# Partial sums kept in the inner tiles of the feed-forward layers, two products of the second tile pair ahead, splits issued in order, lo parts of projection weights by adding transfers

## The chip, the cores and the metric

The kernel runs on one core of a Trainium2 chip (trn2). The metric is the device time of one execution in microseconds (us); lower is better. A run's time is compared by the median of several executions.

## The reference

One inference step of one layer, in float32, over 512 prompt frames and 64 sample frames, which the kernel handles as one matrix of T = 576 tokens with D = 1024 features:

```python
h = layer_norm(ALPHA * x + 0.5 * swiglu_ffn(x, ffn1_w_gu, ffn1_w_down))       # FFN1, LN1
z = h @ w_in            # mLSTM q, k, v, o, i, f | attention q, k, v | gates g_ml, g_att
y_ml  = (normed mLSTM(q, k, v, i, f) * sigmoid(o)) @ w_ml_proj
y_att = band_attention(q, k, v) @ w_att_proj
h = layer_norm(ALPHA * h + (sigmoid(g_ml) * y_ml + sigmoid(g_att) * y_att) @ w_out)   # LN2
y = layer_norm(ALPHA * h + 0.5 * swiglu_ffn(h, ffn2_w_gu, ffn2_w_down))       # FFN2, LN3

def swiglu_ffn(x, w_gu, w_down):
    gate, up = jnp.split(x @ w_gu, 2, axis=-1)
    return (jax.nn.silu(gate) * up) @ w_down          # 2816 hidden features = 22 tiles
```

## The kernel before, in words

**Operands.** Every fp32 operand of a matmul is split in two: `hi`, the operand rounded to the type fp32r, and `lo` = operand − `hi`. A product is three matmuls: hi·hi, hi·lo, lo·hi. ACT makes the `hi` (helper `act`, L137), DVE the `lo` (helper `tt`, L140; `stt`, L143, where a sign is turned).

**Stages.** FFN1, LN1, the projections with the mixers, LN2, FFN2, LN3. The projections run in this order: attention v, k, q for eight pairs of heads (weight tiles 48+j, 40+j, 32+j of `w_in`), attention's gates (64 to 71), its output projection (`ap`), the mLSTM's four heads with eight tiles each (0 to 31), its gates (56 to 63), its output projection (`mp`), the merged output projection (`o`). The tiles `ap`, `mp`, `o` and the gates run back to back on TensorE; between the tiles of the pairs and heads TensorE also runs the mixer.

**Weight stream.** `pump` (L183) keeps a list `plan` of weight tiles of 128x1024. SP loads a raw tile (`wr`, 2 buffers), ACT writes `wh`, DVE writes `wl` = `wr` − `wh` (L213 to 216); `wh` and `wl` have NWB = 4 buffers, so the split of a tile begins when TensorE has finished the tile four before. Four gate/up tiles of FFN2 are split ahead of time by `early` (L172) during the last projection: their `lo` is made by ACT as −hi, and a DMA issued by POOL (L180) adds the raw weights from DRAM onto it (`el`, `eh`).

**The inner tiles of an FFN.** Of the 22 hidden tiles the first two (FFN1) or three (FFN2) are plain. From j = CL on, gate and up tile are made together in Winograd's form of Strassen's scheme (class `Units`, L625): seven products of 12 matmuls of 288 tokens each, in place of eight. Its operands are quarters of the input and sums of them (class `Combos`, `make`, L593: t1 to t4 for four pairs of k-tiles, called as the first unit begins), and quarters of the weights a11, a12, a22 and sums of them s1 to s4 (`prep`). In `run`, the products of one unit j come in this order on TensorE:

- a11·b11 into the PSUM bank X, whose value is copied to `e1` in SBUF,
- a12·b21 into a bank Y; `h` = silu(Y + `e1`) is the gate's first half,
- s2·t2 added onto X, copied to `e2`,
- s1·t1 into Z, s3·t3 onto X, copied to `e3`; `c22` = −`e3` − Z,
- in `finish`, a22·t4 onto X and s4·b22 onto Z, and the rest of the gate and up halves.

The first two products need only the inputs as they are (b11, b21); s2·t2 is the first product that needs a sum of inputs. In the names below `mm_540` is the first unit's bank X in FFN1, `s_495`, `s_512` and so on are hi parts of sums t, `s_496`, `s_513` their lo parts, `tt` the sum itself, `ws`, `wt` the sums of weights, `wu` the raw weights of a unit.

**The down projection.** Output tiles 0 and 1 run together (`joined`), over the hidden tiles that `Hidden.upto` (L762) splits; `get` asks for four ahead.

**What sets the order.** TensorE's order is the program's: `Order.later` puts closures of other work between the matmuls. ACT, DVE, POOL and SP are ordered by a list scheduler with priorities (`hot(n)`, `tc.high_priority(offset=n)`); each of them then runs its list in order.

Of the kernel before, what the change touches and what calls it, by code (L numbers as in the profile page):

```python
# [17 lines left out]
P = 128  # L18
# [63 lines left out]
def tile_layer(ctx: ExitStack, tc: tile.TileContext, ins, outs):  # L82
# [73 lines left out]
    WARM = 8  # L156
    LAST = {1: 6, 2: 6}
    CL = {1: 2, 2: 3}
    NX = 8
    NH0 = 1  # L160
    PIECES = {("in", 48), ("in", 40), ("in", 32)}

    EARLY = [("gu2", j, e) for j in range(2) for e in range(2)]
    CP = (6, 7)
# [4 lines left out]
    wst = {"dma": 0, "conv": 0, "taken": 0, "used": 0, "stop": 0}  # L169
    raws, parts = {}, {}  # L170

    def early(pool, key):  # L172
        c = [k for k, _ in plan].index(key)
        raw = wpool.tile([P, 1024], F32, tag="wr", name=nm("wr"), bufs=2)
        SP.dma_start(raw, plan[c][1])
        hi, lo = parts[c] = tuple(pool.tile([P, 1024], F32R, tag=t, name=nm(t), bufs=len(EARLY)) for t in ("eh", "el"))
        act(hi, raw)

        act(lo, f(hi), scale=-1.0)
        POOL.dma_start(lo, plan[c][1], accum_op=ALU.add)  # L180

    @hot(30)
    def pump(limit=2):  # L183
        while True:
            c = wst["conv"]
            if wst["dma"] < len(plan) and plan[wst["dma"]][0] in EARLY:
                wst["dma"] += 1
                continue
            if c < len(plan) and plan[c][0] in EARLY:
                assert c in parts  # L190
                wst["conv"] += 1
                continue
            if wst["dma"] < min(len(plan), c + 2):
                i = wst["dma"]
                raws[i] = wpool.tile([P, 1024], F32, tag="wr", name=nm("wr"), bufs=2)
                src = plan[i][1]
                SP.dma_start(raws[i][:, :src.shape[1]], src)
                wst["dma"] += 1
                continue
            if c < wst["stop"] and c < wst["taken"] + limit and wst["used"] < NWB:  # L200
                raw = raws.pop(c)
                n = plan[c][1].shape[1]
                hi = wpool.tile([P, 1024], F32R, tag="wh", name=nm("wh"), bufs=NWB)
                if plan[c][0] == "if":

                    r3 = raw[:, :n].rearrange("p (k c) -> p k c", c=64)
                    h3 = hi.rearrange("p (k c) -> p k c", c=P)
                    act(h3[:, :, 0:64], r3)
                    tt(h3[:, :, 64:128], r3, f(h3[:, :, 0:64]), ALU.subtract)
                    parts[c] = (hi, None)  # L210
                else:
                    lo = wpool.tile([P, 1024], F32R, tag="wl", name=nm("wl"), bufs=NWB)
                    step = n if plan[c][0] not in PIECES else 512  # L213
                    for a in range(0, n, step):
                        act(hi[:, a:a + step], raw[:, a:a + step])
                        tt(lo[:, a:a + step], raw[:, a:a + step], f(hi[:, a:a + step]), ALU.subtract)
                    parts[c] = (hi, lo)
                wst["used"] += 1
                wst["conv"] += 1
                continue  # L220
            return
# [411 lines left out]
    class Units:  # L633
# [55 lines left out]
                       skip_group_check=True)  # L689
                od.tick()  # L690

        def copy(self, ps, tag, bufs):
            e = self.pool.tile([P, HT_], F32, tag=tag, name=nm(tag), bufs=bufs)
            act(e, ps)
            return e

        def run(self, tail):
            cur = None
            for j in self.js + [None]:
                new = None  # L700
                if j is not None:
                    new = dict(j=j, X=bank("mm")[:, :HT_], h=self.hr.tile([P, T], F32, tag="h", name=nm("h"), bufs=FT + 1))
                    self.product(new["X"], j, "a11", "b11", True, False)
                    with tc.high_priority(offset=60):
                        new["E1"] = self.copy(new["X"], "e1", 1)
                if cur is not None:
                    self.finish(cur)
                if j is None:
                    return
                h = new["h"]  # L710

                def first(new=new, j=j, h=h):
                    Y = bank("mm")[:, :HT_]
                    self.product(Y, j, "a12", "b21", True, True)
                    with tc.high_priority(offset=60):
                        tt(h[:, :HT_], Y, new["E1"], ALU.add)
                        act(h[:, :HT_], h[:, :HT_], AF.Silu)

                if j < FT - 1:
                    first()  # L720
                else:
                    tail()
                self.prep(j + 1, "a")
                self.prep(j + 1, "s")
                self.product(new["X"], j, "s2", "t2", False, False)
                with tc.high_priority(offset=60):
                    new["E2"] = self.copy(new["X"], "e2", 2)
                self.prep(j + 1, "t")
                Z = new["Z"] = bank("mm")[:, :HT_]
                self.product(Z, j, "s1", "t1", True, False)  # L730
                self.product(new["X"], j, "s3", "t3", False, False)
                with tc.high_priority(offset=60):
                    e3 = self.copy(new["X"], "e3", 1)
                    c = new["c"] = self.pool.tile([P, HT_], F32, tag="c22", name=nm("c22"), bufs=1)
                    stt(c, e3, -1.0, Z, ALU.mult, ALU.subtract)
                self.prep(j + 1, "u")
                if j == FT - 1:
                    first()
                cur = new

        def finish(self, u):
            j, h = u["j"], u["h"]
            self.product(u["X"], j, "a22", "t4", False, True)
            with tc.high_priority(offset=60):
                stt(h[:, :HT_], u["X"], -1.0, h[:, :HT_], ALU.mult, ALU.mult)
            self.prep(j + 1, "b")
            self.load(j + 3)
            self.product(u["Z"], j, "s4", "b22", False, True)
            with tc.high_priority(offset=60):
                tt(h[:, HT_:], u["Z"], u["E2"], ALU.add)  # L750
                act(h[:, HT_:], h[:, HT_:], AF.Silu)
                tt(h[:, HT_:], h[:, HT_:], u["c"], ALU.mult)
            self.hr_done(j, h)

    class Hidden(Act):


        def __init__(self, raw, pools):
            super().__init__()
            self.raw, self.pools = raw, pools  # L760

        def upto(self, k):  # L762
            while len(self.p) <= min(k, FT - 1):
# [1 line left out]
                pool, tag, n = self.pools[(j >= NH0) + (j >= FT // 2)]  # L765
                hi = pool.tile([P, T], F32R, tag=tag, name=nm(tag), bufs=n)
                lo = self.spare if j == FT // 2 - 1 else pool.tile([P, T], F32R, tag=tag, name=nm(tag), bufs=n)
                act(hi, self.raw[j])
                tt(lo, self.raw[j], f(hi), ALU.subtract)
                self.p.append((hi, lo))  # L770

        def get(self, k, hf):
# [829 lines left out]
```

## Time and profile before

| | us |
|---|---|
| median of 3 runs (lowest, highest) | 1629.75 (1627.64, 1630.14) |
| the profiled execution, time | 1625.21 |
| its span on the core | 1623.4 |
| busy: PE, DVE, ACT, POOL | 1585.7, 1082.9, 816.2, 139.0 |
| TensorE's mean granted clock | 0.991 of full |

The span is the time from the first to the last instruction. Busy times are sums over the span; an engine that is less busy than another can still be the one that the other waits for in one place. In the timelines a row's bracket tells how long the engine was idle before it, and what ended that.

### The profile page before, as it was taken

The page shows a single profiled execution, that of the slowest core. Times are in us where ns is not written, and L with a number is a line of the kernel's source. Part 1 is how long each engine was busy: PE and PEld are TensorE (multiplying, and loading weights), DVE is VectorE, ACT ScalarE, POOL GpSimd, SP SyncE. Part 2 cuts the span into 40 slices and gives each one's busy share as a digit, 9 for nine tenths or more (in the row PEclk, how much of TensorE's full clock was granted, in tenths as well). Part 3 has the DMA queues.
Part 4 walks back from the last instruction along what each step waited for, and adds up shares of the span by engine and source line. Part 5 has one row for each costly group of instructions (what it writes and reads, how often), then busy time and mean ns, then how long its engine had stood idle before and what let it go on. Part 6 is the DMA issues. An engine that isn't in the chain of part 4 may idle for free.

```text
span 1623.4 us, 29315 instructions
## 1 busy us (share of the span) xinstructions
PE 1585.7 (98%) x11831; PEld 1561.3 (96%) x11831; DVE 1082.9 (67%) x2154; ACT 816.2 (50%) x1529; POOL 139.0 (9%) x277
## 2 busy tenths in 40 slices
PE   9899999999999999999999999999998999999997
PEld 8899999999999999999999999999998999999996
DVE  7777777635787777673757658434787677766636
ACT  6455456223566566651657476533454455445223
POOL 0000000000313223000101101002110000000001
PEclk9899999999999999999999999999999999999998
DMA  6122231234332333122222122222522232212333
GB/s 217 53 104 104 80 105 46 89 90 124 120 126 87 100 107 102 45 88 85 79 72 79 60 88 64 79 73 84 146 76 78 79 105 93 90 65 85 88 90 116
DMA packets 52896, 148.61 MB, mean 92 GB/s; under 512 B 5784, under 2 KB 16664, under 8 KB 52760
## 3 DMA queue, kind: packets, MB, share of 16 engines
q1 hardware_dynamic: 51608, 144.11, 27.4%
q0 software_dynamic: 576, 2.10, 0.8%
q8 instruction: 93, 1.52, 0.4%
q10 hardware_dynamic: 576, 0.52, 0.1%
q14 instruction: 43, 0.35, 0.1%
HBM read 137.47 MB, written 9.24 MB: 90 GB/s over the span
## 4 chain that ended last, share of the span: by engine, by line
PE 54%; DVE 4%; ACT 1%; issue 1%; DMA 1%; POOL 1%; ACTq 0%; SPq 0%; POOLq 0%; DVEq 0%
PE mm L123 47%; PE aux L123 5%; PE aux L133 1%; DVE s L140 1%; DVE wl L140 1%; DVE s L143 1%; DMA wr<-in_w_gu 1%; ACT wh L137 0%; ACT s L137 0%; DVE tt L140 0%; DMA wr<-in_w_o 0%; DVE dg L140 0%; POOL kh L147 0%; DVE ptl L140 0%; ACT sc L137 0%
## 5 line engine op out<-in xcount | busy, mean ns | idle before, releaser
L123 PE MATMUL mm<-s,wh 128*128 128x288 f32 (+2 forms) x3900 | 799.8, 299 | 13.2 <-ACT s L137 11.5
L123 PEld LDWEIGHTS mm<-s,wh 128*128 128x128 f32 x3900 | 627.9, 190 | 18.4 <-ACT s L137 12.3
L123 PE MATMUL mm<-s,wl 128*128 128x288 f32 (+2 forms) x1934 | 572.4, 296 | 0.0
L123 PEld LDWEIGHTS mm<-s,wl 128*128 128x128 f32 x1934 | 366.5, 189 | 0.0
L140 DVE TENSOR_TENSOR wl<-wr,wh 128x1024 fp32r<-128x1024 f32 (+2 forms) x162 | 192.9, 1195 | 185.3 <-ACT wh L137 184.9
L137 ACT ACTIVATE wh<-wr 128x1024 fp32r<-128x1024 f32 (+2 forms) x163 | 164.7, 1014 | 285.9 <-PE mm L123 267.9
L123 PE MATMUL mm<-h,wh 128*128 128x256 f32 (+1 forms) x672 | 134.5, 294 | 0.0
L140 DVE TENSOR_TENSOR wl<-ws,wh 128x1024 fp32r<-128x1024 f32 x39 | 47.8, 1226 | 112.4 <-ACT wh L137 112.4
L123 PE MATMUL mm<-hc,wh 128*128 128x320 f32 (+1 forms) x560 | 113.7, 295 | 4.8 <-ACT hc L137 2.9
L123 PEld LDWEIGHTS mm<-h,wh 128*128 128x128 f32 x672 | 107.5, 187 | 0.2
L123 PE MATMUL mm<-tx,wh 128*128 128x288 f32 x468 | 98.1, 299 | 1.8 <-ACT e L137 1.8
L123 PE MATMUL mm<-h,wl 128*128 128x256 f32 (+1 forms) x336 | 98.6, 293 | 0.0
L123 PEld LDWEIGHTS mm<-hc,wh 128*128 128x128 f32 x560 | 90.1, 188 | 5.7 <-ACT hc L137 3.4
L137 ACT ACTIVATE wh<-ws 128x1024 fp32r<-128x1024 f32 x39 | 41.2, 1057 | 102.7 <-PE mm L123 102.7
L123 PE MATMUL mm<-hc,wl 128*128 128x256 f32 (+1 forms) x280 | 82.6, 295 | 0.0
L123 PEld LDWEIGHTS mm<-tx,wh 128*128 128x128 f32 x468 | 76.6, 192 | 2.0 <-ACT e L137 2.0
L432 POOL TENSOR_TENSOR rs<-var,mhalf 128x2 f32<-128x2 f32 (+1 forms) x6 | 5.2, 864 | 823.9 <-DVE var L143 428.0
L123 PE MATMUL mm<-tx,wl 128*128 128x288 f32 x234 | 69.9, 299 | 0.0
L123 PEld LDWEIGHTS mm<-h,wl 128*128 128x128 f32 x336 | 62.9, 187 | 0.0
L137 ACT ACT_TABLE_LOAD x45 | 57.7, 1283 | 7.4 <-DVE U L143 4.0
L137 ACT ACTIVATE e<-mm 128x288 f32<-128x288 f32 x117 | 47.3, 404 | 22.6 <-PE mm L123 22.4
L137 ACT ACTIVATE wh<-wu 128x1024 fp32r<-128x1024 f32 x39 | 41.4, 1061 | 31.9 <-PE mm L123 31.9
(297 smaller groups left out, 3061.9 us busy)
## 6 DMA issues: line engine op xcount, KB each, us to landing
wu<-in_w_gu SPq DMA_DIRECT2D x78, 512.0 KB, 4.3
wr<-in_w_in SPq DMA_DIRECT2D x72, 512.0 KB, 3.5
wr<-in_w_dn SPq DMA_DIRECT2D x40, 512.0 KB, 3.5
wr<-in_w_dn SPq DMA_DIRECT2D x20, 384.0 KB, 3.1
G<-in_rbias SPq DMA_DIRECT2D x16, 256.0 KB, 2.8
wr<-in_w_ap SPq DMA_DIRECT2D x8, 512.0 KB, 3.5
wr<-in_w_mp SPq DMA_DIRECT2D x8, 512.0 KB, 3.4
wr<-in_w_o SPq DMA_DIRECT2D x8, 512.0 KB, 3.5
```

What stands on the lines that cost most here:

```text
L123: PE.matmul(out, lhsT, rhs, start=start, stop=stop, **kw)
L133: PE.transpose(out, in_, idn)
L137: ACT.activation(out, in_, func, **kw)
L140: return (eng or DVE).tensor_tensor(out, a, b, op=op)
L143: DVE.scalar_tensor_tensor(out=out, in0=a, scalar=s, in1=b, op0=op0, op1=op1)
L432: return y, POOL.tensor_tensor(y, v, mhalf[:, :n], op=ALU.pow)
```

## The change

1. `add_lo`: for 90 weight tiles (the set `ADDED`: attention's tiles of pairs 2 to 7, the 32 of the mLSTM, the 16 gates, `ap`, `mp`, `o`) `pump` has ACT write `wl` = −`wh` and POOL issue a DMA that adds the raw weights from DRAM, in place of DVE's subtraction.
2. The copies of X go into the halves of `h` and into `c22`, in place of `e1`, `e2`, `e3`; the room goes to two more `tx` tiles of `Combos` (NX = 10 for 8).
3. `begin` and `second`: before s2·t2 of the first unit of each FFN stand a11·b11 and a12·b21 of the second unit, in banks of the tag "aux".
4. `Hidden.upto` chains its splits: the first at high priority, each next one issued after the one before, on ACT and on DVE.

```diff
@@ -156,9 +156,12 @@
...
-    NX = 8
+    NX = 10
     NH0 = 1
     PIECES = {("in", 48), ("in", 40), ("in", 32)}
+
+    ADDED = {("in", c + j) for c in (32, 40, 48) for j in range(2, KT)} | {("in", c) for c in (*range(32), *range(56, 72))} \
+        | {(k, j) for k in ("ap", "mp", "o") for j in range(KT)}
 
...
@@ -169,15 +172,17 @@
...
+    def add_lo(lo, hi, src):
+        act(lo, f(hi), scale=-1.0)
+        POOL.dma_start(lo, src, accum_op=ALU.add)
...
@@ -213,6 +218,9 @@
                     step = n if plan[c][0] not in PIECES else 512
                     for a in range(0, n, step):
                         act(hi[:, a:a + step], raw[:, a:a + step])
+                        if plan[c][0] in ADDED:
+                            add_lo(lo, hi, plan[c][1])
+                            continue
                         tt(lo[:, a:a + step], raw[:, a:a + step], f(hi[:, a:a + step]), ALU.subtract)
                     parts[c] = (hi, lo)
                 wst["used"] += 1
@@ -689,53 +697,57 @@
                        skip_group_check=True)
                 od.tick()
 
-        def copy(self, ps, tag, bufs):
-            e = self.pool.tile([P, HT_], F32, tag=tag, name=nm(tag), bufs=bufs)
+        @hot(60)
+        def copy(self, e, ps):
             act(e, ps)
-            return e
+
+        def begin(self, j, tag="mm"):
+            u = dict(j=j, X=bank(tag)[:, :HT_], h=self.hr.tile([P, T], F32, tag="h", name=nm("h"), bufs=FT + 1), tag=tag)
+            self.product(u["X"], j, "a11", "b11", True, False)
+            self.copy(u["h"][:, :HT_], u["X"])
+            return u
+
+        def second(self, u):
+            h = u["h"][:, :HT_]
+            Y = bank(u["tag"])[:, :HT_]
+            self.product(Y, u["j"], "a12", "b21", True, True)
+            with tc.high_priority(offset=60):
+                tt(h, Y, h, ALU.add)
+                act(h, h, AF.Silu)
 
         def run(self, tail):
-            cur = None
+            cur = ahead = None
             for j in self.js + [None]:
-                new = None
-                if j is not None:
-                    new = dict(j=j, X=bank("mm")[:, :HT_], h=self.hr.tile([P, T], F32, tag="h", name=nm("h"), bufs=FT + 1))
-                    self.product(new["X"], j, "a11", "b11", True, False)
-                    with tc.high_priority(offset=60):
-                        new["E1"] = self.copy(new["X"], "e1", 1)
+                new, ahead = ahead, None
+                if j is not None and new is None:
+                    new = self.begin(j)
                 if cur is not None:
                     self.finish(cur)
                 if j is None:
                     return
-                h = new["h"]
-
-                def first(new=new, j=j, h=h):
-                    Y = bank("mm")[:, :HT_]
-                    self.product(Y, j, "a12", "b21", True, True)
-                    with tc.high_priority(offset=60):
-                        tt(h[:, :HT_], Y, new["E1"], ALU.add)
-                        act(h[:, :HT_], h[:, :HT_], AF.Silu)
-
-                if j < FT - 1:
-                    first()
-                else:
+                if j == FT - 1:
                     tail()
+                elif new["tag"] == "mm":
+                    self.second(new)
                 self.prep(j + 1, "a")
+                if j == self.js[0]:
+
+                    ahead = self.begin(j + 1, "aux")
+                    self.second(ahead)
                 self.prep(j + 1, "s")
                 self.product(new["X"], j, "s2", "t2", False, False)
-                with tc.high_priority(offset=60):
-                    new["E2"] = self.copy(new["X"], "e2", 2)
+                self.copy(new["h"][:, HT_:], new["X"])
                 self.prep(j + 1, "t")
                 Z = new["Z"] = bank("mm")[:, :HT_]
                 self.product(Z, j, "s1", "t1", True, False)
                 self.product(new["X"], j, "s3", "t3", False, False)
+                c = new["c"] = self.pool.tile([P, HT_], F32, tag="c22", name=nm("c22"), bufs=1)
+                self.copy(c, new["X"])
                 with tc.high_priority(offset=60):
-                    e3 = self.copy(new["X"], "e3", 1)
-                    c = new["c"] = self.pool.tile([P, HT_], F32, tag="c22", name=nm("c22"), bufs=1)
-                    stt(c, e3, -1.0, Z, ALU.mult, ALU.subtract)
+                    stt(c, c, -1.0, Z, ALU.mult, ALU.subtract)
                 self.prep(j + 1, "u")
                 if j == FT - 1:
-                    first()
+                    self.second(new)
                 cur = new
 
         def finish(self, u):
@@ -747,7 +759,7 @@
             self.load(j + 3)
             self.product(u["Z"], j, "s4", "b22", False, True)
             with tc.high_priority(offset=60):
-                tt(h[:, HT_:], u["Z"], u["E2"], ALU.add)
+                tt(h[:, HT_:], u["Z"], h[:, HT_:], ALU.add)
                 act(h[:, HT_:], h[:, HT_:], AF.Silu)
                 tt(h[:, HT_:], h[:, HT_:], u["c"], ALU.mult)
             self.hr_done(j, h)
@@ -757,7 +769,7 @@
...
         def upto(self, k):
             while len(self.p) <= min(k, FT - 1):
@@ -765,8 +777,13 @@
                 pool, tag, n = self.pools[(j >= NH0) + (j >= FT // 2)]
                 hi = pool.tile([P, T], F32R, tag=tag, name=nm(tag), bufs=n)
                 lo = self.spare if j == FT // 2 - 1 else pool.tile([P, T], F32R, tag=tag, name=nm(tag), bufs=n)
-                act(hi, self.raw[j])
-                tt(lo, self.raw[j], f(hi), ALU.subtract)
+
+                a, b = self.prev
+                with tc.issue_after(a.ins) if j else tc.high_priority(offset=100):
+                    a = ACT.activation(hi, self.raw[j], AF.Copy)
+                with tc.issue_after(b.ins) if j else tc.high_priority(offset=100):
+                    b = tt(lo, self.raw[j], f(hi), ALU.subtract)
+                self.prev = a, b
                 self.p.append((hi, lo))
 
         def get(self, k, hf):
```

**TensorE at the start of FFN1's first unit.** `mm_556` and `mm_555` are the bank Y of the first unit, `mm_540` its X. Before:

```order
L123 MATMUL mm_556<-s_75,wh_413 128x288
L123 MATMUL mm_556<-s_76,wh_413 128x288
L123 MATMUL mm_556<-s_75,wl_414 128x288
L123 MATMUL mm_540<-tx_405,wh_525 128x288
L123 MATMUL mm_540<-tx_406,wh_525 128x288
L123 MATMUL mm_540<-tx_405,wl_526 128x288
```

With the change (`aux_574` and `aux_589` are X and Y of the second unit; the rows between the two pieces go on in the same way):

```order
L123 MATMUL mm_555<-s_76,wh_413 128x288
L123 MATMUL mm_555<-s_75,wl_414 128x288
L123 MATMUL aux_574<-s_77,wh_570 128x288
L123 MATMUL aux_574<-s_78,wh_570 128x288
L123 MATMUL aux_574<-s_77,wl_571 128x288
L123 MATMUL aux_574<-s_79,wh_570 128x288
```

```order
L123 MATMUL aux_589<-s_75,wh_570 128x288
L123 MATMUL aux_589<-s_76,wh_570 128x288
L123 MATMUL aux_589<-s_75,wl_571 128x288
L123 MATMUL mm_540<-tx_405,wh_525 128x288
L123 MATMUL mm_540<-tx_406,wh_525 128x288
L123 MATMUL mm_540<-tx_405,wl_526 128x288
```

24 matmuls stand between a12·b21 and s2·t2 of the first unit that stood behind it before; their operands `s_77`, `s_69` are parts of the input itself, `wh_570` and `wl_571` the second unit's a12 and a11.

**DVE at the same place.** Before, the last of its rows being the lo part of the last t2 (`s_513`):

```order
L140 TENSOR_TENSOR wt_576<-ws_575,wu_393 128x512
L140 TENSOR_TENSOR s_496<-tt_486,s_495 128x288
L140 TENSOR_TENSOR wt_576<-wt_576,wu_393 128x512
L140 TENSOR_TENSOR tt_503<-s_96 128x288
L140 TENSOR_TENSOR tt_503<-s_92,s_96 128x288
L140 TENSOR_TENSOR h_304<-h_304,mm_443 128x320
L140 TENSOR_TENSOR wl_595<-wt_576,wh_594 128x1024
L143 SCALAR_TENSOR_TENSOR s_505<-tt_503,s_504 128x288
L140 TENSOR_TENSOR s_505<-tt_503,s_504 128x288
L140 TENSOR_TENSOR tt_503<-s_92,tt_503 128x288
L140 TENSOR_TENSOR tt_503<-tt_503,s_92 128x288
L143 SCALAR_TENSOR_TENSOR s_513<-tt_503,s_512 128x288
```

With the change:

```order
L140 TENSOR_TENSOR h_541<-mm_555,h_541 128x288
L140 TENSOR_TENSOR tt_503<-s_96 128x288
L140 TENSOR_TENSOR tt_503<-s_92,s_96 128x288
L140 TENSOR_TENSOR wt_605<-ws_604,wu_393 128x512
L143 SCALAR_TENSOR_TENSOR s_505<-tt_503,s_504 128x288
L140 TENSOR_TENSOR s_505<-tt_503,s_504 128x288
L140 TENSOR_TENSOR h_575<-aux_589,h_575 128x288
L140 TENSOR_TENSOR tt_503<-s_92,tt_503 128x288
L140 TENSOR_TENSOR wt_605<-wt_605,wu_393 128x512
L143 SCALAR_TENSOR_TENSOR s_513<-tt_503,s_512 128x288
L140 TENSOR_TENSOR tt_503<-tt_503,s_92 128x288
L140 TENSOR_TENSOR wl_623<-wt_605,wh_622 128x1024
```

The lo part of s2 and s4 (`wl_595`, now `wl_623`) moved from ahead of the last two sums to behind them, the sum for t4 moved behind t2's lo part, and `h_575`, the second unit's h, came in; further up, the second unit's `wl_571` moved ahead of the sum of weights `ws`.

**ACT in the last projection.** `wh` from `wr` with the rows `eh`, `el` are the hi parts of `o` tiles between the early tiles of FFN2; `sq` are squares for LN2. Before, the end of it:

```order
L137 ACTIVATE wh_14039<-wr_13887 128x1024
L137 ACTIVATE sq_13951<-s_13837 128x320
L137 ACTIVATE eh_13933<-wr_13931 128x1024
L137 ACTIVATE el_13934<-eh_13933 128x1024
L137 ACTIVATE sq_13989<-s_13915 128x256
L137 ACTIVATE wh_14108<-wr_13965 128x1024
L137 ACTIVATE sq_14029<-s_13915 128x320
L137 ACTIVATE eh_14020<-wr_14018 128x1024
L137 ACTIVATE el_14021<-eh_14020 128x1024
L137 ACTIVATE sq_14065<-s_13993 128x256
L137 ACTIVATE wh_14365<-wr_14112 128x1024
```

With the change:

```order
L137 ACTIVATE wh_14067<-wr_13914 128x1024
L137 ACTIVATE sq_13978<-s_13863 128x320
L137 ACTIVATE wl_14068<-wh_14067 128x1024
L137 ACTIVATE sq_14017<-s_13942 128x256
L137 ACTIVATE eh_14048<-wr_14046 128x1024
L137 ACTIVATE el_14049<-eh_14048 128x1024
L137 ACTIVATE wh_14137<-wr_13993 128x1024
L137 ACTIVATE sq_14057<-s_13942 128x320
L137 ACTIVATE wl_14138<-wh_14137 128x1024
L137 ACTIVATE sq_14094<-s_14021 128x256
L137 ACTIVATE wh_14395<-wr_14142 128x1024
```

Each `wh` of an `o` tile is followed by a `wl` from `wh`, and the last tile's `wh` (`wh_14137`, before `wh_14108`) moved from ahead of the last early tile's `eh` and `el` to behind them. POOL's adding transfers follow in the same order.

## Rows read from the trace of the kernel before

**Rows 1.** The page's busy times, shares of the span and instructions of each engine:

```profile
PE 1585.7 (98%) x11831; PEld 1561.3 (96%) x11831; DVE 1082.9 (67%) x2154; ACT 816.2 (50%) x1529; POOL 139.0 (9%) x277
```

**Rows 2.** Windows, inside FFN1: length, busy us (count) by engine, granted clock, DMA share, GB/s:

```profile
60.00:250.00 190.00, 190.00 (x1432) 189.54 (x1431) 140.93 (x206) 96.94 (x154) 0.00 (x0) 1.00 0.27 94
```

**Rows 3.** Windows at the units' and down projections' starts, one of them (273.20) at half clock:

```profile
33.20:60.00 26.80, 18.28 (x116) 17.03 (x115) 20.53 (x37) 11.68 (x22) 0.00 (x0) 0.81 0.13 49
268.00:280.00 12.00, 9.57 (x59) 9.11 (x58) 10.73 (x18) 9.99 (x16) 0.00 (x0) 0.86 0.30 90
273.20:276.60 3.40, 3.40 (x16) 3.40 (x15) 3.40 (x6) 3.06 (x5) 0.00 (x0) 0.50 0.29 104
1244.00:1265.00 21.00, 15.01 (x93) 14.42 (x92) 15.59 (x29) 8.17 (x16) 0.00 (x0) 0.84 0.11 46
1464.60:1476.60 12.00, 9.59 (x71) 9.16 (x70) 10.73 (x17) 10.07 (x17) 0.00 (x0) 1.00 0.29 85
```

**Rows 4.** Timeline of PE, first unit of FFN1: start us, us, instruction [idle before]:

```profile
36.33 0.29 PE L123 MATMUL mm<-s,wl 128*128 128x288 f32 x1
38.37 0.53 PE L123 MATMUL mm<-tx,wh 128*128 128x288 f32 x2 [1.76 <-ACT e L137]
...
47.15 1.19 PE L123 MATMUL mm<-s,wh 128*128 128x288 f32 x2 [5.89 <-ACT s L137]
```

**Rows 5.** Timeline of DVE there:

```profile
36.82 0.45 DVE L143 SCALAR_TENSOR_TENSOR s<-tt,s 128x288 fp32r<-128x288 f32 x1
...
37.56 1.22 DVE L140 TENSOR_TENSOR ws<-wu 128x1024 f32<-128x1024 f32 x1
...
41.30 0.68 DVE L140 TENSOR_TENSOR wt<-ws,wu 128x512 f32<-128x512 f32 x1
...
47.21 0.46 DVE L143 SCALAR_TENSOR_TENSOR s<-tt,s 128x288 fp32r<-128x288 f32 x1
```

**Rows 6.** Timeline of ACT there:

```profile
36.98 1.04 ACT L137 ACTIVATE wh<-wu 128x1024 fp32r<-128x1024 f32 x1
```

**Rows 7.** Timeline of PE, first unit of FFN2:

```profile
1253.55 0.61 PE L123 MATMUL mm<-s,wh 128*128 128x288 f32 x1 [5.40 <-ACT s L137]
1254.75 0.61 PE L123 MATMUL mm<-s,wh 128*128 128x288 f32 x1 [0.60 <-DVE s L143]
```

**Rows 8.** Timeline of DVE there:

```profile
1245.99 0.45 DVE L140 TENSOR_TENSOR tt<-s,tt 128x288 f32<-128x288 f32 x1
...
1254.25 0.45 DVE L143 SCALAR_TENSOR_TENSOR s<-tt,s 128x288 fp32r<-128x288 f32 x1
```

**Rows 9.** Timeline of all engines before the first down projection:

```profile
267.94 0.75 DVE L140 TENSOR_TENSOR h<-h,h 128x576 fp32r<-128x576 f32 x1
...
268.78 0.69 ACT L137 ACTIVATE h<-h 128x576 fp32r<-128x576 f32 x1 [1.78 <-DVE h L140]
```

**Rows 10.** The early tiles' lo parts (`el`): ns min/median/max, first and last start:

```profile
L137 ACT ACTIVATE el<-eh x4: 1046/1056/1061, 1156.0 to 1178.9; 128x1024 fp32r<-128x1024 f32 x4
L180 POOL DMA_DIRECT2D el<-in_w_gu x4: 844/862/1061, 1157.7 to 1180.2; - x4
...
DMA to landing us min/median/max: 5.5/6.7/7.5
```

**Rows 11.** DMA queues in 1155 to 1190, share of 16 engines:

```profile
q1 hardware_dynamic: 1296, 4.72, 39.3%
q0 software_dynamic: 576, 2.10, 36.4%
```

**Rows 12.** Timeline of ACT in the projection `mp`:

```profile
1116.65 1.06 ACT L137 ACTIVATE wh<-wr 128x1024 fp32r<-128x1024 f32 x1 [1.67 <-PE mm L123]
```

**Rows 13.** Timeline of ACT in the projection `o`:

```profile
1177.79 1.06 ACT L137 ACTIVATE eh<-wr 128x1024 fp32r<-128x1024 f32 x1 [0.27 <-DMA wr<-in_w_gu]
```

**Rows 14.** Timeline of PE in `o`, first use of the last tile's lo part:

```profile
1186.66 0.28 PE L123 MATMUL aux<-mg,wl 128*128 128x256 f32 x1
```

**Rows 15.** Waits of PE within attention, 425 to 675: total, times, longest:

```profile
PE aux L133 <- DVE ptl L140: 1.8, 6, 0.3
```

More of the change, by code (lines that the diff above doesn't have):

```diff
@@ L177, in early @@
         act(hi, raw)
-        act(lo, f(hi), scale=-1.0)
-        POOL.dma_start(lo, plan[c][1], accum_op=ALU.add)
+        add_lo(lo, hi, plan[c][1])
     @hot(30)
@@ L215, in pump @@
                         act(hi[:, a:a + step], raw[:, a:a + step])
+                        if plan[c][0] in ADDED:
+                            add_lo(lo, hi, plan[c][1])
+                            continue
                         tt(lo[:, a:a + step], raw[:, a:a + step], f(hi[:, a:a + step]), ALU.subtract)
@@ L759, in __init__ @@
             super().__init__()
-            self.raw, self.pools = raw, pools
+            self.raw, self.pools, self.prev = raw, pools, (None, None)
         def upto(self, k):
```

## The prediction

> **What bounds the kernel now.** I read the busy times first: TensorE is busy 1585.7 of 1623.4 us, and every other engine has a third of its time or more left [rows 1]. So only two things can save time here, fewer matmuls or fewer TensorE gaps; the change keeps the number of matmuls. Next come the windows by stage. Inside an FFN TensorE is busy 190.00 of 190.00 us with 1432 matmuls, 0.1327 us each, so that a product of 12 takes 1.59 us [rows 2]; with no gap there, nothing that the change gives ACT or DVE in that stretch can count. The gaps lie at the starts [rows 3]: a window's length less its matmuls at 0.1327 us gives a loss of 26.8 − 15.4 = 11.4 us at FFN1's first unit, 21.0 − 12.3 = 8.7 at FFN2's, 12.0 − 7.8 = 4.2 and 12.0 − 9.4 = 2.6 at the two down projections. That is 26.9 us in all, and the most that parts 2 to 4 can gain.
>
> The timeline of TensorE tells what the first two wait for. In FFN1 it waits 5.89 us until 47.15 for a hi part of a sum [rows 4], the last t2; in FFN2 5.40 us until 1253.55 for the same, then 0.60 for its lo part [rows 7]. DVE makes these sums and works without a break there: two short instructions of 0.45 us take 0.74 together, so rows overlap by 0.08, and an instruction costs 0.37 (288 elements), 0.60 (512) or 1.14 (1024) [rows 5], and by proportion 0.33 (256) and 0.41 (320).
>
> **Two products ahead, FFN1.** TensorE is through with Y at 36.5 [rows 4]. The second unit's `wh` is ready at 38.02 [rows 6]. DVE's list of the change gives its `wl`: from 36.82 two sums (0.74), an h of 320 (0.41), a `tt` (0.37), so it begins at 38.34 and ends at 39.56, 1.22 later [rows 5]. Two of the 24 matmuls run before that, 22 take 2.92, the nine of s2·t2 that wait for nothing 1.19: 43.7. The lo part of the last t2 begins after 38.34 + 2 x 1.14 + 2 x 0.60 + 10 x 0.37 = 45.52 (the rows of the list from `wl_571` to `wt_605`), where it began at 47.21 [rows 5], and ends at 45.97. Three matmuls later, at 46.3, TensorE has done 36 matmuls (4.78 us) since 36.5: a loss of 5.0 for 11.4. Gain 6.4; I take **6.0**, since a little of the 11.4 lies ahead of 36.5. Bounds: 3.2 (the two products fill 2 x 1.59 us of the wait and nothing else improves) and 8.
>
> **The same, FFN2.** TensorE's wait began at 1253.55 − 5.40 = 1248.15 [rows 7], nine matmuls after Y, which ended at 1246.9. DVE's list of the change from 1245.99 [rows 8]: six short instructions (2.18), then `wl` from 1248.17 to 1249.39; 22 + 9 matmuls end at 1253.5. The lo part of the last t2 begins at 1245.99 + 12 x 0.37 + 0.33 + 0.41 + 2 x 1.14 = 1253.45 (1254.25 before [rows 8]) and ends at 1253.9; TensorE is through at 1254.2, a loss of 7.3 − 4.8 = 2.5 for 8.7. Gain 6.2; I take **5.2**, one less, because TensorE still rests 2.2 us for `wl` and the clock may fall as it did before. Bounds again 3.2 and 8.
>
> **The clock.** Granted clock was 0.81 and 0.84 over these two windows, and one level, 0.50 of full (1.2 of 2.4 GHz), for 3.40 us after the first down projection's waits [rows 3], where half of the stretch, 1.7 us, is lost. After equal waits at the second it stayed 1.00, and the two losses differ by 1.6. So the same rest is followed by a fall in one place and by none in another: I count falls as a bound of 1.7 each, not as a certainty. The Trainium skill, "TensorE: Matmul & The Clock Gate", section "What's actually happening", calls the throttled clock the default that activity has to release. [...]
>
> **Partial sums in the halves of h, two more tx.** As many copies and additions as before: nothing on ACT or DVE, hidden by a TensorE that never waits in [rows 2]. 0, within 0.5 either way.
>
> **Splits in order.** Before FFN1's down projection ACT spends 0.69 and DVE 0.75 on a split of a hidden tile that `joined` needs late [rows 9]; in the change the first ones needed come first. ACT's `hc` comes about 0.5 us earlier at each down projection, of a loss of 4.2 and 2.6: **1.0** in all, bounds 0 and 2.5; late next is DVE's lo part of the same tile.
>
> **Lo parts by adding transfers.** 90 subtractions of DVE (1.14 each) go; ACT gets 90 x 1.06, POOL 90 issues of 0.86 [rows 10]. ACT has half its time left, POOL nine tenths [rows 1]. What counts is lateness. The chain is hi 1.06, −hi 1.06, issue 0.86, 6.7 to landing [rows 10]: 9.7 us at most. In the back-to-back projections the split of a tile starts when TensorE ends the tile four before [rows 12], so three tiles of 48 x 0.1327 = 6.37 us stand between: 19.1. 9.4 us are left; the cost is 0. SP's raw tile is freed earlier, after ACT's hi and not DVE's lo. DMA engines: four adds of 2.10 MB took 36.4% of 35 us, 3.2 us each; 4.72 MB of plain loads 39.3%, 1.5 us per 512 KB [rows 11]. A tile then needs 4.7 of 6.37 us.
>
> One place is tight: the end of `o`, where the early tiles of FFN2 go through the same queues. The last `o` tile's hi now stands behind the last early tile's hi and −hi on ACT, and its add behind that tile's add on POOL. From 1177.79, the early hi of before [rows 13], or some 1.5 us earlier because raws are freed sooner: four activations of 1.06 and one of squares, 0.45, to 1181.0, then issue and landing 6.7 to 7.5 [rows 10]: 1187.7 to 1188.5, for a use at 1186.66 [rows 14]. DMA load there rises too: 26.5 us of 35 are taken [rows 11], and three more adds of 3.2 us would fill them. I charge **−1.5**, bounds 0 and −5.
>
> In the mixers TensorE waits for DVE in small pieces (ptl 1.8 us over six times between 425 and 675 [rows 15]); DVE relieved could give some of it back, ACT loaded could add to it: 0, from −4 to +4.
>
> **Sum.** 6.0 + 5.2 + 1.0 − 1.5 = 10.7 us off the profiled execution's 1625.21: 1614.5. The median of the runs lies 4.5 above that execution, so I forecast **1619** as the median.
>
> **The rivals.**
> - *The wait only shifts*: the two products fill 2 x 1.59 us per FFN, but the sums come as late as before and the clock falls as before. Gain 6.4, less 1.5 in `o`: 1625. For it: DVE has no gap in [rows 5], and whatever is put first delays something. Against: by the list the s2/s4 subtraction (1.14) really stands behind the last t2 now.
> - *The clock falls after every rest that is left*: the two units and both down projections. One fall at the down projections and one of the units' is in the forecast already (4.2 less 1.0, and the one taken off FFN2); falls at FFN1's unit and at the second down projection, 1.7 each, and 0.7 more at FFN2's make 4.1: 1623. For it: the 1.76 us rest ahead of 38.37 [rows 4] stays much the same. Against: 1.00 in the last window of [rows 3]. [...]
> - *ACT's extra work delays the mixers*: if each of six pairs and four heads has one chain that an added −hi of 1.06 us holds up, 10.6 us come back: 1629.7, no change. Against: ACT is half idle [rows 1], and the waits there are for DVE [rows 15].
> - *Adding transfers cannot keep up*, the slower side. It decides once an add costs the DMA engines more than 6.37 − 1.5 = 4.9 us, or it lands more than 9.4 us later than reckoned above. If it cost twice the measured 3.2, a tile would take 7.9 us, and 40 back-to-back tiles (16 gates, 8 each of `ap`, `mp`, `o`) would lose 1.5 each: 60 us, 1679. For it: an add costs twice a load in [rows 11] and lands after up to 7.5 us. Against: four of them ran beside nine plain loads within 76% of the engines' time there. The Trainium skill, "SBUF — State Buffer", section "SBUF: two separate sides", speaks against this change: POOL cannot write descriptors while DVE holds their shared port in its fast mode. By that page an issue would stretch by the length of such a DVE instruction; the four issues of 0.84 to 1.06 us [rows 10] differ by 0.2 only, and no row tells in which mode DVE ran beside them.
> - *The relief of DVE counts in the mixers*: +4 there, or bounds of 8 at the units: 1610 to 1613.
> - *It does not do what it says*: the listings show that the products and the splits are moved; the relief of DVE in the projections is real but on an engine that TensorE waits for almost nowhere. This is in the forecast: I give part 1 no gain.
>
> **How the numbers follow.** Forecast (1613 to 1622) 0.58; falls of the clock 0.08; shifted wait 0.11; delayed mixers 0.09; late adds 0.07; more gain 0.07. 0.2%, about what can be told from no change, is 3.3 us, so "same" is 1626.5 to 1633. Faster takes forecast, falls, shifted wait and more gain: 0.84; same the delayed mixers and a mild case of late adds: 0.10; slower 0.06. The range must hold 0.8: 1611 to 1627 takes forecast, falls, shifted wait and some of the last; its upper end is also the sum with all its lower bounds in the units (3.2 + 3.2 − 1.5 = 4.9 off, 1625) and one clock fall.
>
> **What would show it.** Right: at FFN1's first unit 24 matmuls into `aux` before s2·t2, last t2 at about 45.5 us, the two unit windows losing about 5 and 3 us; the down projections' first waits half a microsecond shorter; no TensorE wait for a `wl` in the projections except one of 1 to 3 us at the last `o` tile. Wrong: waits of TensorE for `wl` by DMA in `ap`, the gates or `mp`; a tile pitch above 6.4 us there; half clock after the products ahead; or attention and mLSTM stretches longer than before by a microsecond per pair.

## The result

The changed kernel takes 1631.57 us in the median (1627.82 to 1633.14, 12 runs) and the kernel before 1628.12 (1625.02 to 1630.14, 12 runs). The ratio is 1.0019 with a 95% interval of 1.001 to 1.0028: slower by 3.5 us, where 10.7 faster was forecast. The profiled execution took 1632.4 us (span 1630.6), 0.8 above its median; that of before lay 2.9 below its own, so the two traces differ by 7.2 us.

The page's busy times, against [rows 1], and its DMA queues (packets, MB, share of the 16 engines; before, q0 had 576 packets and 0.8%):

```profile
PE 1589.6 (97%) x11831; PEld 1565.9 (96%) x11831; DVE 983.0 (60%) x2064; ACT 887.6 (54%) x1611; POOL 202.6 (12%) x367
...
q1 hardware_dynamic: 51608, 144.11, 27.1%
q0 software_dynamic: 13536, 49.29, 18.6%
```

DVE lost 100 us and ACT gained 71, as meant; TensorE does the same work. The same place in that work can be looked up in both traces by the columns that ran before it; the start of the matmul there tells where the time went (in the rows "second unit" the order of the products differs, so it is the same amount of work and another product):

| same place in TensorE's work, us | before | after | after − before |
|---|---|---|---|
| last of FFN1's plain tiles | 35.27 | 35.23 | 0.0 |
| second unit of FFN1 | 56.49 | 51.39 | −5.1 |
| in FFN1's down projection | 288.51 | 282.24 | −6.3 |
| start of attention | 433.95 | 427.58 | −6.4 |
| end of attention | 683.74 | 676.11 | −7.6 |
| in `o`, its fifth tile | 1166.32 | 1159.03 | −7.3 |
| after `o` | 1207.90 | 1216.58 | +8.7 |
| second unit of FFN2 | 1264.90 | 1270.33 | +5.4 |
| in FFN2's down projection | 1485.80 | 1492.79 | +7.0 |

So the change gained 7.6 us up to the end of attention and 3.3 at FFN2's first units, and lost 16.0 at the end of `o`, in a stretch that took 41.6 us before; 1.6 more went at FFN2's down projection. TensorE's waits of the changed kernel (the engine, for what, total, times, longest), whole span:

```profile
PE aux L123 <- DMA wl<-in_w_o: 5.7, 1, 5.7
PE mm L123 <- DMA wl<-in_w_o: 4.3, 1, 4.3
PE aux L123 <- DVE wl L140: 3.2, 2, 2.2
PE mm L123 <- ACT hc L783: 2.7, 2, 1.4
PE mm L123 <- ACT c L137: 2.6, 2, 1.3
...
PE mm L123 <- DVE hc L140: 1.9, 2, 1.0
PE mm L123 <- ACT s L137: 1.5, 1, 1.5
```

The first two lines are 10.0 us of waiting for the lo parts of two `o` tiles. The windows show what follows such waits (columns as in [rows 2]):

```profile
33.20:60.00 26.80, 21.51 (x154) 20.36 (x153) 22.80 (x39) 13.39 (x24) 0.00 (x0) 1.00 0.20 78
263.00:275.00 12.00, 9.64 (x71) 9.19 (x71) 10.24 (x16) 10.51 (x18) 0.00 (x0) 1.00 0.33 103
1182.00:1187.00 5.00, 5.00 (x23) 5.00 (x24) 3.76 (x8) 3.84 (x6) 1.72 (x2) 0.50 0.89 210
1193.00:1204.50 11.50, 11.39 (x68) 11.34 (x69) 3.96 (x9) 1.99 (x4) 2.42 (x3) 0.79 0.01 2
1252.70:1273.70 21.00, 17.53 (x118) 16.91 (x117) 18.43 (x34) 10.01 (x18) 0.00 (x0) 0.92 0.12 48
1470.40:1482.40 12.00, 9.79 (x62) 9.36 (x61) 10.41 (x16) 11.03 (x19) 0.00 (x0) 0.86 0.30 89
```

After the first wait TensorE ran 5.0 us at half clock, 2.5 lost; after the second the clock was 0.79 over 11.5 us, another 2.4. Waits and clock make 14.9 of the 16.0.

**How two tiles come late.** From the timelines of SP, ACT, POOL and PE at the end of `o` (start us, us, instruction, idle before):

```profile
1170.17 0.33 SPq L202 DMA_DIRECT2D wr<-in_w_o  x1
1172.21 0.33 SPq L182 DMA_DIRECT2D wr<-in_w_gu  x1
```

```profile
1169.09 1.06 ACT L137 ACTIVATE eh<-wr 128x1024 fp32r<-128x1024 f32 x1 [5.22 <-DMA wr<-in_w_gu]
...
1171.15 1.04 ACT L137 ACTIVATE wh<-wr 128x1024 fp32r<-128x1024 f32 x1
...
1179.66 1.06 ACT L137 ACTIVATE eh<-wr 128x1024 fp32r<-128x1024 f32 x1 [5.00 <-DMA wr<-in_w_gu]
...
1181.71 1.04 ACT L137 ACTIVATE wh<-wr 128x1024 fp32r<-128x1024 f32 x1
...
1183.02 1.04 ACT L137 ACTIVATE wl<-wh 128x1024 fp32r<-128x1024 f32 x1
```

```profile
1182.10 0.86 POOL L177 DMA_DIRECT2D el<-in_w_gu  x1 [7.45 <-ACT el L137]
1184.35 0.86 POOL L177 DMA_DIRECT2D wl<-in_w_o  x1 [1.39 <-ACT wl L137]
```

```profile
1181.93 0.58 PE L123 MATMUL mm<-mg,wl 128*128 128x256 f32 x1 [4.28 <-DMA wl<-in_w_o]
...
1193.11 0.58 PE L123 MATMUL aux<-mg,wl 128*128 128x256 f32 x1 [5.69 <-DMA wl<-in_w_o]
```

Follow the last early tile. Its raw load is issued at 1172.21, when the hi of an `o` tile, begun at 1171.15, has freed the buffer. It lands 7.4 us later: ACT stood idle 5.00 us for it until 1179.66. Only then come its hi, its −hi, and the last `o` tile's hi (1181.71) and −hi (1183.02), since ACT runs its list in order; POOL issues the add at 1184.35, it lands after 8.8 us, and TensorE goes on at 1193.11. Forecast were 1181.0 for the issue and 6.7 to 7.5 us of landing [rows 10]; since TensorE was 7.3 us ahead of the old trace here (the table), 1181.0 stands for 1173.7 in this one, and the issue came 10.7 us late.

So the loads go round in a ring: an early load waits for a raw buffer, the buffer for an `o` tile's hi, that hi for the early hi ahead of it on ACT, and that one for its own load. Seen from ACT, the last three early loads took 8.9, 7.6 and 7.4 us, one after the other.

### The profile page after: what moved, and what is told of

Same layout as the page of the kernel before. It is cut to its first block, busy times and chain, and to the rows that moved or that the text cites. A ratio compares the mean times of both kernels' runs of the same rounds, so it can differ in the third digit from the quotient of the medians.

```text
span 1630.6 us, 29396 instructions
## 1 busy us (share of the span) xinstructions
PE 1589.6 (97%) x11831; PEld 1565.9 (96%) x11831; DVE 983.0 (60%) x2064; ACT 887.6 (54%) x1611; POOL 202.6 (12%) x367
## 3 DMA queue, kind: packets, MB, share of 16 engines
q0 software_dynamic: 13536, 49.29, 18.6%
## 4 chain that ended last, share of the span: by engine, by line
PE 86%; DVE 6%; DMA 3%; ACT 3%; issue 2%; SPq 0%; POOL 0%; ACTq 0%; DVEq 0%; POOLq 0%
PE mm L123 74%; PE aux L123 10%; PE aux L133 2%; DMA wr<-in_w_gu 2%; DVE wl L140 1%; ACT wh L137 1%; DVE s L140 1%; DVE s L143 1%; DVE tt L140 1%; DVE sc L1074 1%; ACT sc L137 0%; DMA wr<-in_w_dn 0%; ACT s L137 0%; ACT L137 0%; DMA w<-in_w_gu 0%
## 5 line engine op out<-in xcount | busy, mean ns | idle before, releaser
L123 PE MATMUL mm<-s,wh 128*128 128x320 f32 (+2 forms) x3700 | 758.1, 299 | 2.2 <-ACT s L137 1.5
L123 PEld LDWEIGHTS mm<-s,wh 128*128 128x128 f32 x3700 | 594.9, 190 | 6.5 <-ACT s L137 1.8
L123 PE MATMUL mm<-s,wl 128*128 128x320 f32 (+2 forms) x1834 | 542.5, 296 | 0.0
L123 PEld LDWEIGHTS mm<-s,wl 128*128 128x128 f32 x1834 | 347.2, 189 | 0.0
L140 DVE TENSOR_TENSOR wl<-wr,wh 128x1024 fp32r<-128x1024 f32 (+2 forms) x72 | 78.7, 1102 | 104.0 <-ACT wh L137 104.0
L123 PE MATMUL mm<-tx,wh 128*128 128x288 f32 x604 | 123.5, 295 | 0.0
L123 PEld LDWEIGHTS mm<-tx,wh 128*128 128x128 f32 x604 | 97.3, 189 | 0.0
L137 ACT ACTIVATE wl<-wh 128x1024 fp32r<-128x1024 f32 x90 | 94.9, 1054 | 0.8
L123 PE MATMUL mm<-tx,wl 128*128 128x288 f32 x302 | 89.4, 296 | 0.0
L177 POOL DMA_DIRECT2D wl<-in_w_in x66 | 57.9, 878 | 245.5 <-ACT wl L137 169.8
```

The lines of the kernel that those rows point to most:

```text
L123: PE.matmul(out, lhsT, rhs, start=start, stop=stop, **kw)
L137: ACT.activation(out, in_, func, **kw)
L140: return (eng or DVE).tensor_tensor(out, a, b, op=op)
L177: POOL.dma_start(lo, src, accum_op=ALU.add)
```

## The experiments

Two questions were open: what makes the `o` tiles late, and what each other part is worth.

**No adds in `o`.** In `ADDED`:

```diff
-        | {(k, j) for k in ("ap", "mp", "o") for j in range(KT)}
+        | {(k, j) for k in ("ap", "mp") for j in range(KT)}
```

> The changed kernel with the eight tiles of the last projection (o) split as before, their lo parts by DVE; the other 82 adding transfers stay. Theory Q (the o tiles' adds and the early tiles' adds together fill the DMA queues, raw loads take 7.5 us, the last two o tiles come late): both waits for wl in o (4.3 and 5.7 us) and the half clock after them go, 16.3 us come back: about 1615 us, TensorE's stretch from the end of mp to FFN2 as long as before. Rival P (adding transfers delay TensorE wherever they stand, o only shows it): less than half comes back, about 1625 us or more, and waits for wl appear in other places.

Measured: 1615.39 us, ratio to before 0.9913 (0.9896 to 0.993), 16.2 below the changed kernel. That is theory Q's number; no wait for a `wl` by DMA is left. Both kernels are beaten.

**No adds at all.** `if plan[c][0] in ADDED:` becomes `if False:`.

> The changed kernel with no adding transfers for the projections (DVE makes all 90 lo parts), so parts 2 to 4 alone. Theory Q: the gains at the two units (5.1 and 3.3 us) and about 0.5 of the down projections stay, o as before, attention as before (1.3 us of gain lost): about 1616.5 us, 1 to 2 us above the kernel without o's adds. Rival P: faster than that kernel by several us, 1610 or less.

Measured: 1619.62, ratio 0.9945 (0.993 to 0.996). The adds outside `o` are worth 4.2 us between these two kernels, a gain: rival P falls. The time is also 3 above the expected 1616.5; in the trace attention's waits for ptl are 3.0 us, where they were 1.8 before [rows 15].

**The adds alone**, on the kernel before (`ADDED` and the four lines of the test in `pump`).

> The kernel before with the 90 adding transfers and nothing else of the change. Theory Q: o loses 16 us as in the changed kernel, attention gains about 1.3: about 1643 us, 15 above before, with the same two waits of 4 to 6 us for wl of o. Rival M (the late tiles come from the other parts, which changed the scheduler's order in o): o loses under 5 us, 1633 or less.

Measured: 1639.69, ratio 1.0065 (1.005 to 1.008). Its TensorE waits:

```profile
PE aux L123 <- DMA wl<-in_w_o: 6.7, 1, 6.7
PE mm L123 <- DMA wl<-in_w_o: 4.1, 1, 4.1
```

The same two waits come without any other part of the change: rival M falls. The total is 11 above before, not 15.

**The same without `o`**: the first edit on that kernel.

> The kernel before with the adding transfers for the 82 tiles other than o, nothing else of the change. From the run with all 90 on the kernel before: attention's first pairs lose 2.5 us by waits for the row maxima, the later ones gain 3.6 by waits for ptl and vc that go: 1628 us, no difference to before beyond 2 us, no wait for a wl. Rival P (adding transfers cost wherever they stand): 1631 or more.

Measured: 1626.41, ratio 0.9987 (0.9978 to 0.9997): 1.9 us faster, no wait for a `wl`.

**Early tiles by DVE.** In `early`:

```diff
-        add_lo(lo, hi, plan[c][1])
+        tt(lo, raw, f(hi), ALU.subtract)
```

> The changed kernel with all adding transfers for o, but with the lo parts of the four early tiles of FFN2 by DVE's subtraction. Theory Q: four adds fewer on the queues while the o tiles' adds run, raw loads back to 4 to 5 us, both waits nearly gone (under 2 us in all): 1615 to 1618 us. Rival A (the o tiles' splits stand behind the early tiles' activations on ACT, transfers are not the matter): ACT is freed of 4 x 1.06 us only, and at least 8 us of the 16 stay: 1623 us or more.

Measured: 1616.45, ratio 0.9927 (0.9909 to 0.9945): 15 of the 16 us come back, one wait of 1.3 us stays. ACT has four −hi fewer to make, but its order of hi parts was the same, each early tile's ahead of an `o` tile's. Queues and landing times of the changed kernel in 1140 to 1195:

```profile
q0 software_dynamic: 1406, 5.10, 52.9%
...
wr<-in_w_gu SPq DMA_DIRECT2D x6, 512.0 KB, 5.4
wl<-in_w_o POOLq DMA_DIRECT2D x5, 512.0 KB, 8.1
el<-in_w_gu POOLq DMA_DIRECT2D x4, 512.0 KB, 7.9
```

and with the early tiles by DVE, in 1135 to 1190:

```profile
q0 software_dynamic: 944, 3.41, 35.2%
...
wl<-in_w_o POOLq DMA_DIRECT2D x6, 512.0 KB, 6.1
wr<-in_w_gu SPq DMA_DIRECT2D x6, 512.0 KB, 4.0
```

With four adds fewer the raw loads land in 4.0 and not 5.4 us in the median, the adds in 6.1 and not 8. The adds' queue takes 35% of the engines' time, not 53%. The last early load was no faster, though; it was issued 8.9 us sooner:

```profile
1163.28 1.13 SPq L182 DMA_DIRECT2D wr<-in_w_gu  x1
```

```profile
1171.40 1.06 ACT L137 ACTIVATE eh<-wr 128x1024 fp32r<-128x1024 f32 x1 [6.18 <-DMA wr<-in_w_gu]
```

Seen from ACT it took 8.1 us, and the two before it 4.0 and 4.7 in place of 8.9 and 7.6: most of what the last one gained comes round the ring from these two.

**Half of the `o` tiles**: `("o", j)` for j in range(4), the tiles that are split ahead of the early ones.

> The changed kernel with adding transfers for the first four o tiles only (and all other 82); tiles 4 to 7 by DVE. If the trouble is the meeting of the o tiles' adds with the early tiles' adds and loads, and not adds in o as such: as good as without any add in o, 1614 to 1617 us, no wait for a wl of o. If o's adds cost by themselves: half of the 16 us stay, 1621 to 1624.

Measured: 1614.25, ratio 0.9913 (0.9898 to 0.9928). So the four adds that come before the early tiles cost nothing; the loss is in the meeting of the others with the early tiles' adds and loads.

**Early tiles 3.5 us later**, which turns the order on ACT and POOL round for the last three `o` tiles:

```diff
-        later(2000 + 7000 * i, lambda key=key: early(epool, key))
+        later(5500 + 7000 * i, lambda key=key: early(epool, key))
```

> The changed kernel, all adding transfers kept, with the four early tiles of FFN2 begun 3.5 us later in the program's order, so that from the last but two o tile on an o tile's hi and -hi stand ahead of the early tile's on ACT and its add ahead on POOL. Theory A (in-order ACT: the o tiles' splits wait behind an early tile whose raw load takes 7.5 us): both waits for wl of o go or shrink to under 2 us in all, about 1616 us. Theory L (load alone: twelve adds and twelve loads are more than the DMA engines can do in that stretch, whatever the order): at least 6 us of the 10 us of waits stay, 1624 us or more.

Measured: 1623.71, ratio 0.997 (0.9957 to 0.9983). Its wait:

```profile
PE aux L123 <- DMA wl<-in_w_o: 6.2, 1, 6.2
```

The first wait is gone, the last tile's stays at 6.2 us. Half of the loss goes with that order. The other half does not show a loss without the ring: the last `o` tile's hi, now behind the third early tile's, still came after a slow load that ACT was idle for,

```profile
1170.97 1.06 ACT L137 ACTIVATE eh<-wr 128x1024 fp32r<-128x1024 f32 x1 [4.66 <-DMA wr<-in_w_gu]
```

so neither theory holds alone.

**A raw buffer of its own for the early tiles**, everything else as in the changed kernel:

```diff
-        raw = wpool.tile([P, 1024], F32, tag="wr", name=nm("wr"), bufs=2)
+        raw = pool.tile([P, 1024], F32, tag="er", name=nm("er"), bufs=1)
```

> The changed kernel, all adds kept and the same order on ACT and POOL, but the early tiles' raw loads get a buffer of their own in place of the two that they share with the o tiles. Theory C (chain: each early raw load starts only when an o tile's hi has been made and the other way round, so each late load makes the next one later): at least half of the 16 us comes back, 1623 or less. Theory L (load alone: the DMA engines have more than they can do there): the waits for wl of o stay at 8 us or more in all, 1628 or more.

Measured: 1621.29, ratio 0.9957 (0.994 to 0.9974): 10 of the 16 us come back, with the same adds and the same order on ACT and POOL. Its wait, and its queue in 1140 to 1195:

```profile
PE aux L123 <- DMA wl<-in_w_o: 3.1, 1, 3.1
```

```profile
q0 software_dynamic: 1388, 5.03, 49.3%
...
er<-in_w_gu SPq DMA_DIRECT2D x4, 512.0 KB, 7.6
```

The loads are as slow as ever (7.6 us), yet most of the loss is gone: what made it large was the ring through two raw buffers, in which an early load could not start before an `o` tile's hi was made and that hi stood behind the early load before. What remains was not taken apart; the early loads still wait for each other there, through their one buffer.

**Without the two products ahead**, on the kernel without adds in `o`: `if j == self.js[0]:` becomes `if False:`.

> The kernel without adding transfers for o (1615.4 us), and without the two products ahead at the first units. Theory F (the products fill the wait, the scheduler's order brings the sums 1.7 and 0.8 us sooner only because of them, and they cost a new wait of 1.3 us for the copy c): the units' waits for the last t2 are 5 to 6 us again, the waits for c go: 8 to 10 us lost, about 1624. Rival S (the sums come sooner through the other edits, the products fill little): under 4 us lost, 1619 or less.

Measured: 1622.92, ratio to before 0.9969 (0.9958 to 0.998), 7.5 above the kernel that it was made from. Waits:

```profile
PE mm L123 <- ACT s L137: 11.2, 3, 5.6
```

The waits for s are those of before again (11.5 us there), the waits for the copy c are gone: theory F, at a little less than the 8 to 10 us that it gave.

**Hidden splits as before**, on the same kernel (the diff's last hunk undone).

> The kernel without adding transfers for o (1615.4 us), with the hidden tiles' splits as before (no high priority, no chain). Forecast was 0.5 us for each down projection: 1616.4. Rival (the first wait there ends with ACT's last activation of the inner tiles, whatever order the splits have): no difference, 1615 to 1616, both first waits within 0.2 us.

Measured: 1616.87, ratio 0.9931 (0.9916 to 0.9945), against 1615.39 and 0.9913: the intervals overlap. The first waits of TensorE in the two down projections sum to the same:

```profile
PE mm L123 <- ACT hc L137: 2.6, 2, 1.3
```

2.7 with the splits in order, 2.6 without. No wait is shorter by that order, and 1.5 us between the medians is within the spread; more on it below.

**Attention's adds from pair 3**, on the same kernel (`range(3, KT)` in `ADDED`).

> The kernel without adds for o (1615.4 us), its attention adds beginning with pair 3 in place of 2. The first pairs' waits for the row maxima (mx, 1.3 us over two) should shrink to the 0.8 us of before and 0.5 to 1 us come back: 1614.5. Rival: the wait moves on to the next pair, 1615.4 or more.

Measured: 1615.44, ratio 0.9921 (0.9906 to 0.9935): no difference in time. In the trace the wait did shrink, from 1.3 us to

```profile
PE aux L133 <- DVE mx L1074: 0.8, 2, 0.6
```

so it did not move on to the next pair, but half a microsecond is below what the runs tell.

## Why the prediction was wrong, step by step

**The term of `o` failed, and with it the sign.** The prediction put the place, the order on ACT and POOL and the direction right ("I charge −1.5, bounds 0 and −5") and the size wrong by a factor of ten: 16.0 in the trace, 16.2 between medians. Four things were wrong or left out. It took the last early hi "some 1.5 us earlier" than [rows 13]; it came 1.9 later on the clock of the trace, 9.2 later as seen from TensorE. The raw loads were reckoned at their old times although the same paragraph says that three more adds would fill the engines. It looked at the last tile only, where the one before was late as well. And it priced lateness as lateness, without the half clock after it, which the prediction itself had found elsewhere. The experiments tell what it takes. Against the kernel before, the stretch of the table around the end of `o` is longer in the traces by 16.0 us here and 15.7 with the adds alone, by 8.3 with the early tiles later, 5.9 with a raw buffer of their own, 1.5 with their lo parts by DVE, 0.4 with half of the `o` tiles and 0.0 without adds in `o`; the medians say the same. So it takes both: slow loads cost 6 us without the shared buffers, the shared buffers 1.5 with faster loads, and together, with an engine that runs its list in order and so makes each late load the start of the next, 16.

**The units were right but for a new wait.** Forecast for the last t2's lo part in FFN1: 45.52. The timelines of DVE and PE there:

```profile
45.35 0.45 DVE L143 SCALAR_TENSOR_TENSOR s<-tt,s 128x288 fp32r<-128x288 f32 x1
```

```profile
39.46 0.40 PE L123 MATMUL aux<-s,wl 128*128 128x288 f32 x1 [1.02 <-DVE wl L140]
...
45.35 0.90 PE L123 MATMUL mm<-s,wh 128*128 128x288 f32 x2 [1.53 <-ACT s L137]
...
50.88 0.53 PE L123 MATMUL mm<-tx,ah 128*128 128x288 f32 x2 [1.31 <-ACT c L137]
```

It began at 45.35, and `wl` ended the second wait near the forecast 39.56. But the loss of the window is 26.8 − 154 x 0.1327 = 6.4, not 5.0: at 50.88 stands a wait of 1.31 us for the copy c. Before, a11·b11 of the next unit stood between s3·t3 and a22·t4, which write the same bank X; now that product has been taken ahead, and a22·t4 waits until ACT has copied X (without the products ahead these waits are gone, above). The prediction counted the copies as hidden "by a TensorE that never waits" and did not ask what the moved products had covered where they came from. FFN2 has the same 1.31, and its clock fell after the wait for `wl` (0.92 over 21 us, 1.7 lost): 21.0 − 118 x 0.1327 = 5.3, for a forecast of 2.5, which these two explain. Gains by the windows: 11.4 − 6.4 = 5.0 and 8.7 − 5.3 = 3.4, forecast 6.0 and 5.2. In FFN1 the waits got shorter by 3.1 us (8.3 before, 5.2 now); the rest goes with the clock, 0.81 of full before [rows 3] and 1.00 now. In FFN2 six traces with the products ahead and no fall of the clock there gained 4.5 to 4.7, near the forecast. The 3.2 us of waits for `wl` among TensorE's waits are the second unit's (1.02 at 39.46, 2.15 in FFN2), as reckoned; for the last t2 1.5 are left of 5.89 and 5.40 [rows 4, 7].

**The clock** came and went, as bounded: after the first down projection's waits it stayed at 1.00 (0.86 over that window before [rows 3]), after the second it fell to 0.86 (1.00 before), 1.6 us gained and 1.2 lost. The rival in which it falls after every rest that is left is refuted by the first of these windows. Whether the falls have nothing to do with the change is open: in 12 us around these waits the clock was 0.86 in 7 of 8 places in the four traces without splits in order, and in 6 of 18 in the nine traces with them, after waits of nearly the same length. That order may make falls rarer, at 1.2 to 1.6 us each; no experiment was made to tell.

**Splits in order: no shorter wait, where 1.0 was forecast.** The first waits at the down projections are 1.39 and 1.27 us for 1.47 before, and the run without that order has the same. They still end with ACT's `hc`. In FFN1 it begins at 265.90, right behind a weight tile's `wh` (264.94, 1.06 us), as it does at 270.65 in the kernel before (`wh` at 269.71), and that is not what the order changes.

**Adding transfers elsewhere: 0 forecast, 2 to 4 gained.** Chain and load were reckoned right: 18.6% of the span for 94 adds is 3.2 us each, and they land in time:

```profile
L177 POOL DMA_DIRECT2D wl<-in_w_in x66: 853/865/1061, 442.8 to 1067.0; - x66
...
DMA to landing us min/median/max: 5.3/5.7/9.4
```

Of the rival in which they "cannot keep up" only the meeting place came true; the back-to-back tiles kept their pitch, 491 matmuls in the 65 us from 1075 on in either kernel. The Trainium skill, "SBUF — State Buffer", section "SBUF: two separate sides", says that DVE in its fast (two-port) mode keeps POOL from writing descriptors. The issue times show no sign of it, 0.85 to 1.06 us with DVE busy 60% of the span, as in [rows 10]; but in which mode DVE ran no run tells, so the rule is neither shown nor refuted here.

The gain lies in attention. Between the table's two rows there, eight traces with the adds are 2.5 to 3.1 us shorter than before, three in which the clock fell there, the changed kernel's among them, 1.3, and the one without adds is 1.1 longer. From there to the end of the mLSTM's tiles all took the same time to 0.1 us: relief of DVE is worth nothing there. The waits of [rows 15] for ptl are gone, but two for the row maxima (mx) are 0.5 us longer in the first pair, where ACT makes −hi ahead of them; with the adds from pair 3 on they are not. One of 0.8 us came in at 663. The rival "delayed mixers" is refuted.

## What to carry to other kernels

When work is moved to a shared queue, look for the stretch where that queue's users meet, and follow the whole ring there: a load that waits for a buffer, that waits for an engine in order, that waits for the load before. Reckon such a ring with the new landing times and not with those of the old trace, and add the clock that a late operand costs. And of a product that is moved ahead, ask what its old place covered.

## What the runs showed of the hardware

An adding transfer of 512 KB takes 3.2 us of the DMA engines' time and a plain load 1.5 [rows 11]; the add's landing time ranged from 5.3 us to 9.4, and that of plain loads in the changed kernel from 3.5 in the median of 1140 to 1190 to 7.6 beside two adds. The DMA share alone does not tell trouble. In the windows of the changed kernel

```profile
1075.00:1140.00 65.00, 65.00 (x491) 65.00 (x491) 13.20 (x30) 28.45 (x40) 20.71 (x25) 1.00 0.79 165
1155.00:1175.00 20.00, 19.29 (x147) 19.05 (x146) 10.54 (x28) 10.20 (x14) 3.45 (x4) 1.00 0.78 170
1175.00:1185.00 10.00, 5.72 (x37) 5.52 (x36) 2.81 (x8) 5.30 (x7) 1.51 (x2) 0.79 0.90 200
```

the DMA engines are busy 79% of 65 us without a TensorE wait, and a share of 78 to 90% some microseconds on goes with the 10 us of waits.
